# The second half of an output projection by Strassen's products

## The chip, the cores and the metric

One core of one Trainium2 chip runs the whole program in one launch. The metric is device time in microseconds (us) of that core; lower is better. An execution's time is what the device needs for the launch; the span of a profile goes from the first to the last instruction and is a little shorter.

Five engines work side by side, each in the order of its own queue: TensorE (PE; its weight loads are listed as PEld), VectorE (DVE), ScalarE (ACT), GpSimd (POOL) and SyncE (SP), which here only issues DMA transfers. Matmuls write their results into PSUM banks of 512 columns of 4 bytes for 128 partitions; the other engines take them from there.

## What is computed

A decoder trunk of two layers on 512 tokens with 1024 channels, all in float32. Layer 1, where the change is (shortened):

```python
xn = rms_norm(h, norm_mix[1])
proj = gelu(xn @ w_in_odd)                      # 512 x 2048
u, v = proj[:, :1024], proj[:, 1024:]
mix = u * gate(v)                               # position mixing in chunks of 128
h = h + mix @ w_out_odd                         # 512x1024 by 1024x1024: the change is here
hn = rms_norm(h, norm_ffn[1])
h = h + gated_conv_ffn(hn, w_ffn_gate[1], w_ffn_up[1], conv_ffn[1], b_conv_ffn[1], w_ffn_down[1])
out = rms_norm(h, final_norm)
```

## The kernel before

The residual h lies in SBUF as eight tiles `h[0]` to `h[7]` of 128 channels by 512 tokens. A float32 product is made of three matmuls in a rounded format (`fp32r`): each operand is split into a high part (rounded, by ScalarE) and a low part (the rest, by VectorE), and high x high, high x low and low x high are summed in one bank (`mm3`, lines 156 to 159). `parts` (line 149) splits weights in this way. `summed` (line 138) makes the low part in another way: ScalarE writes the negated high part, and a DMA issued by GpSimd adds the raw values onto it.

`mixer1` (line 898) makes layer 1's mixer. Its last steps are these. The group "u1" multiplies the second half of u (banks of 128 tokens by 512 channels); along with it `spatial`, `gated` and `turned` make the gated mix of a head (128 channels) and transpose it on TensorE. `turned(j)` (line 1099) takes the transposed bank, `mT`, into a high part (ScalarE, line 1108) and a low part (VectorE, line 1109) of a tile `mx`: `mix[j]` is channel block j by 512 tokens. Blocks 0 to 3 are turned within "u1", blocks 4 to 7 within the first half of the output projection by the hook `second_half` (line 1163).

The output projection "oo" is one call of `project` (line 303). It makes two halves: half 0 gives `h[0..3]`, half 1 gives `h[4..7]`. A half takes four raw tiles of weights (256 rows by 512 columns each), split by `parts`, and makes 4 row blocks x 8 chunks of the contraction x 3 matmuls = 96 matmuls of 512 columns. For the first four chunks the row blocks alternate, for the last four each row block is finished by itself (`group`, line 161). A finished row block is added to `h[k]` by VectorE (line 315), and `norm.add(k)` prepares it for the FFN: the high and the low part `hg[k]` of h times the gain (ScalarE line 202, VectorE line 203), the square (ScalarE), and the sum of squares (GpSimd, line 213).

Behind it `ffn1` starts: `Ffn.pair_weights` (line 631) fetches and splits four tiles of gate and up weights, `direct` (line 645) multiplies them with `hg` in the order 0, 4, 1, 5, 2, 6, 3, 7, and `turn_residual` (line 1184) transposes h on TensorE for the last part of the kernel (`hT`, two tiles ahead of each pair of row blocks). Meanwhile `block_sums` and `prepare` make the operands of the first feature pair that goes by Strassen's products; the kernel already uses these in its other layers' steps, with `multiply` (line 558) and the table `BANK` (line 554), which says which products go on in one bank.

Buffers that matter here, each a set of slots that come free when the last reader is done: raw weights (tag `raw`, 4), their high and low parts (`whi`, `wlo`, 6 each), PSUM banks for matmuls (7), tag `v` in mixer1 (4 tiles of 2 x 512 columns: first v, then the gated mix `gt`), tag `u` (2), `vn` (4, at the end `mx`), `ws` (1).

The order of the work on each engine is set by a planner at build time: it takes, of what it reckons ready, the instruction that stands first in the program. `behind(a, b)` (line 83) puts a behind b on their engine. Each queue is then strict; a transfer on SP's queue that waits for a slot holds up the transfers behind it.

Of the kernel before, what the change touches and what calls it, by code (L numbers as in the profile page):

```python
# [31 lines left out]
def tile_trunk(ctx: ExitStack, tc: tile.TileContext, x, norm_mix, norm_ffn, final_norm,  # L32
# [3 lines left out]
    nc = tc.nc  # L36
    x = x[0]
# [92 lines left out]
    def fetch(src, a, b, name):  # L130
        raw = wp.tile([P, a, b], F32, tag="raw", bufs=4, name=f"raw_{name}")
        nc.sync.dma_start(raw, src)
        return raw, a, b, name
# [15 lines left out]
    def parts(raw, a, b, name, after=(None, None)):  # L149
        hi = wp.tile([P, a, b], F32R, tag="whi", bufs=6, name=f"whi_{name}")  # L150
        lo = wp.tile([P, a, b], F32R, tag="wlo", bufs=6, name=f"wlo_{name}")
        behind(nc.scalar.activation(hi, raw, AF.Copy), after[1])  # L152
        behind(nc.vector.tensor_tensor(lo, raw, hi.bitcast(F32), ALU.subtract), after[0])  # L153
        return hi, lo
# [31 lines left out]
    h = [cp.tile([P, S], F32, tag=f"h{k}", name=f"h{k}") for k in range(NK)]  # L186
# [116 lines left out]
    def project(name, w, acts, ks, norm, before=None, halves=(0, 1), tail=4):  # L303

        for gi in halves:
            chunks = half_weights(name, w, ks, gi)

            def lhs(k, j):
                hi, lo, n = chunks[k]
                cs = slice(j * P, (j + 1) * P)  # L310
                return hi[:, n, cs], lo[:, n, cs]

            def done(j, ps):
                k = gi * 4 + j
                nc.vector.tensor_tensor(h[k], ps, h[k], ALU.add)  # L315
                if norm is not None:
                    norm.add(k)

            group(f"{name}{gi}", range(4), ks, lhs, lambda k, j: acts[k], tail, done,
                  before if gi == 0 else None)  # L320
# [221 lines left out]

    STEPS = [(0, None, True), (2, (0, 2, 0), False), (4, (0, 2, 1), True)]
    for f in range(6, NF, 4):
        STEPS += [(f, (f - 4, f, 0), False), (f + 2, (f - 4, f, 1), f + 4 < NF)]
# [44 lines left out]
    class Ffn:  # L592
# [38 lines left out]
        def pair_weights(self, order):  # L631

            ch = {}
            for key, half in order:
                name = f"{key}{self.layer}_0_{half}"
                raw = wp.tile([P, 4, 2 * P], F32, tag="raw", bufs=4, name=f"raw_{name}")
                w = (w_ffn_gate if key == "g" else w_ffn_up)[self.layer][:, : 2 * P]
                w = w.rearrange("(h k p) c -> p h k c", h=2, p=P)
                for h_ in range(2):
                    nc.sync.dma_start(raw.rearrange("p (k h) c -> p h k c", h=2)[:, h_],  # L640
                                      w[:, h_, 2 * half : 2 * half + 2])
                ch[key, half] = parts(raw, 4, 2 * P, name)
            return ch

        def direct(self, ch, before):
# [56 lines left out]
        def moving(self, product, kp):  # L702

            if product in (1, 2, 3):
                k = kp if product == 1 else kp + NP
                c = slice(HALF, S) if product == 3 else slice(0, HALF)
                return hg[k][0][:, c], hg[k][1][:, c]
            if product in (6, 7):
                t = self.t23[kp][product - 6]
                return t[:, 0, :], t[:, 1, :]  # L710
            return tuple(t[:, {4: 0, 5: 1}[product], :] for t in self.t41[kp])
# [186 lines left out]
    def mixer1(norm):  # L898
        w = w_in_odd[0]
        with tc.tile_pool(name="m1", bufs=1) as mp:  # L900
# [74 lines left out]
            class InProducts:  # L975
# [19 lines left out]
                def put(self, product, how, at):  # L995
                    self.stat[product] = [how(raw, 2, 512, f"{self.name}_{product}_{n}")
                                          for n, raw in enumerate(self.raw[at])]
# [75 lines left out]
                                                   op0=ALU.mult, op1=ALU.subtract)  # L1073
                vn.append((hi, lo))

            u, gt, mix = {}, {}, {}

            def by_chunk(ap):
                return ap.rearrange("p (n c) -> p n c", c=P)
# [19 lines left out]
            def turned(j):  # L1099
                half, i = j // 4, j % 4  # L1100
                if i == 0:
                    mix["t", half] = [mp.tile([P, 4, S], F32R, tag="vn", bufs=4,
                                              name=f"mx{half}_{n}") for n in range(2)]
                ps = mm_bank(f"mT{j}")
                for t in range(NT):
                    nc.tensor.transpose(ps[:, t * P : (t + 1) * P], gt[j][:, t, :], ident)
                hi, lo = (x[:, i, :] for x in mix["t", half])
                nc.scalar.activation(hi, ps, AF.Copy)
                nc.vector.tensor_tensor(lo, ps, hi.bitcast(F32), ALU.subtract)
                mix[j] = hi, lo  # L1110

            u[0] = mp.tile([P, NT, S], F32, tag="u", bufs=2, name="u0")

# [49 lines left out]
            def second_half(k):  # L1163
                if 1 <= k < 4:
                    for j in ((4,), (5,), (6, 7))[k - 1]:
                        turned(j)

            nxt = Norm("f1", lambda k: prm1("ffn", k))
            project("oo", w_out_odd[0], mix, list(range(NK)), nxt, before=second_half)
            return nxt  # L1170


# [241 lines left out]
    n = ffn0(n)  # L1414
# [32 lines left out]
```

## Time and profile before

| | us |
|---|---|
| median of three runs | 972.78 (971.95 to 972.93) |
| profiled execution | 972.66 |
| its span, first to last instruction | 970.9 |
| TensorE busy in the span | 961.0 (99%) |
| VectorE busy | 812.9 (84%) |
| ScalarE busy | 597.5 (62%) |
| GpSimd busy | 152.0 (16%) |

The granted TensorE clock was 0.998 over the span. Times in the trace count from the start of the span. A row of the timeline shows start, duration, engine, line, operation, the tile written and the tiles read; in square brackets how long the engine sat idle before it, and what ended that. A row of grouped instructions shows the count, busy time and the mean of one in nanoseconds, or minimum, median and maximum. Rows of waits show who waited for whom: total, times, longest. In the table by stretches stand for each engine the busy time and the number of instructions. The durations of matmuls overlap: what counts is the distance from one start to the next.

### The profile page before, as it was taken

The numbers are of one execution on the slowest core, as the hardware profiler recorded it, in microseconds if no ns is written. First come the engines' busy times: TensorE is split into PE (matmuls) and PEld (weight loads), VectorE is DVE, ScalarE is ACT, GpSimd is POOL, SyncE is SP. The second block draws the span as 40 slices with busy tenths as digits, with TensorE's granted clock in tenths as the row PEclk, the third lists the DMA queues.
The fourth block names the chain that finished last, engine by engine and source line by source line (L and its number), as shares of the span: only waits on it lengthen the run. The fifth ranks groups of instructions, "written<-read, shape, count | busy, mean of one in ns | idle before, by whom it ended". The sixth has DMA issues, their size and how long they took to land.

```text
span 970.9 us, 13658 instructions
## 1 busy us (share of the span) xinstructions
PE 961.0 (99%) x4952; PEld 818.6 (84%) x4952; DVE 812.9 (84%) x1387; ACT 597.5 (62%) x895; POOL 152.0 (16%) x173
## 2 busy tenths in 40 slices
PE   9999999999999999999999999999999999999996
PEld 7888888988888888888888888889888888888885
DVE  6887458999898998998878675589998989889897
ACT  5523347765675665765586834587665666656775
POOL 3141023110111010110311001221111011100123
PEclk9999999999999999999999999999999999999999
DMA  7442225776777677774352333167767777668775
GB/s 252 149 137 86 87 88 111 178 180 161 195 175 168 157 174 195 168 176 135 128 153 87 109 109 108 51 136 182 185 142 196 195 174 174 159 162 200 195 154 139
DMA packets 92335, 148.33 MB, mean 153 GB/s; under 512 B 5124, under 2 KB 56300, under 8 KB 92268
## 3 DMA queue, kind: packets, MB, share of 16 engines
q1 hardware_dynamic: 76236, 98.69, 32.1%
q0 software_dynamic: 14256, 46.93, 26.8%
q10 hardware_dynamic: 1776, 1.84, 0.6%
q8 instruction: 39, 0.64, 0.3%
q14 instruction: 28, 0.23, 0.1%
HBM read 98.42 MB, written 2.10 MB: 104 GB/s over the span
## 4 chain that ended last, share of the span: by engine, by line
PE 94%; DVE 3%; DMA 1%; issue 1%; ACT 0%; POOLq 0%; DVEq 0%; POOL 0%
PE dn L158 3%; PE dn L159 3%; PE dn L157 3%; PE d L158 3%; PE d L157 3%; PE d L159 3%; PE vu_a L1026 2%; PE gu L157 2%; PE gu L159 2%; PE oo L159 2%; PE oo L157 2%; PE gu L158 2%; PE oe L159 1%; PE oe L158 1%; PE oo L158 1%; PE oe L157 1%
## 5 line engine op out<-in xcount | busy, mean ns | idle before, releaser
L144 POOL DMA_DIRECT2D wlo_g<-raw_g x20 | 17.2, 862 | 318.8 <-ACT wlo_g L142 118.3
L617 DVE SCALAR_TENSOR_TENSOR c<-rows,prm,c 128x512 f32<-128x512 f32 x88 | 65.3, 744 | 1.6 <-ACT c L615 1.4
L158 PE MATMUL dn<-wlo_dn,a_hi 128*128 128x512 f32 x144 | 56.2, 390 | 0.0
L158 PE MATMUL d<-a_lo,whi_d 128*128 128x512 f32 x144 | 56.2, 390 | 0.0
L159 PE MATMUL dn<-whi_dn,a_lo 128*128 128x512 f32 x144 | 56.2, 390 | 0.0
L159 PE MATMUL d<-a_hi,wlo_d 128*128 128x512 f32 x144 | 56.1, 390 | 0.0
L157 PE MATMUL d<-a_hi,whi_d 128*128 128x512 f32 x144 | 56.1, 390 | 0.0
L157 PE MATMUL dn<-whi_dn,a_hi 128*128 128x512 f32 x144 | 56.1, 390 | 0.0
L731 ACT ACTIVATE whi_a<-raw_g 128x512 fp32r<-128x512 f32 x20 | 12.6, 632 | 61.3 <-PE g_10e L571 9.0
L213 POOL TENSOR_TENSOR ssq_f<-ssq_f,sq_f 128x512 f32<-128x512 f32 x14 | 19.8, 1411 | 142.4 <-issue 102.0
L142 ACT ACTIVATE wlo_g<-raw_g 128x1024 fp32r<-128x1024 f32 x20 | 21.2, 1062 | 27.5 <-PE g_2e L581 8.8
L202 ACT ACTIVATE hg<-h,prm 128x512 fp32r<-128x512 f32 x24 | 17.3, 721 | 33.1 <-DVE h L315 33.1
L615 ACT ACTIVATE c<-rows,prm 128x512 f32<-128x512 f32 x44 | 31.4, 715 | 9.8 <-DVE rows L828 9.6
L625 ACT ACTIVATE s<-c,prm 128x512 f32<-128x512 f32 x44 | 31.4, 716 | 6.2 <-DVE c L617 6.1
L1201 DVE SCALAR_TENSOR_TENSOR y<-dn,small,y 128x512 f32<-128x512 f32 x40 | 28.0, 749 | 8.1 <-PE dn L159 8.1
L203 DVE SCALAR_TENSOR_TENSOR hg<-h,prm,hg 128x512 fp32r<-128x512 f32 x24 | 22.6, 944 | 11.9 <-ACT hg L202 11.9
L159 PEld LDWEIGHTS dn<-whi_dn,a_lo 128*128 128x128 f32 x144 | 27.0, 188 | 5.7
L159 PEld LDWEIGHTS d<-a_hi,wlo_d 128*128 128x128 f32 x144 | 27.0, 188 | 5.7
L153 DVE TENSOR_TENSOR wlo_dn<-raw_dn,whi_dn 128x1024 fp32r<-128x1024 f32 x18 | 22.0, 1224 | 11.7 <-ACT whi_dn L152 10.6
L157 PEld LDWEIGHTS d<-a_hi,whi_d 128*128 128x128 f32 x144 | 27.1, 188 | 5.4
L157 PEld LDWEIGHTS dn<-whi_dn,a_hi 128*128 128x128 f32 x144 | 27.1, 188 | 5.4
L158 PEld LDWEIGHTS dn<-wlo_dn,a_hi 128*128 128x128 f32 x144 | 27.0, 188 | 5.4
(1060 smaller groups left out, 3261.6 us busy)
## 6 DMA issues: line engine op xcount, KB each, us to landing
raw_g<-in_w_ffn_gate_dram SPq DMA_DIRECT2D x40, 512.0 KB, 3.8
raw_u<-in_w_ffn_up_dram SPq DMA_DIRECT2D x40, 512.0 KB, 4.3
raw_dn<-in_w_ffn_down_dram SPq DMA_DIRECT2D x22, 512.0 KB, 6.0
wlo_g<-raw_g POOLq DMA_DIRECT2D x20, 512.0 KB, 4.6
wlo_u<-raw_u POOLq DMA_DIRECT2D x20, 512.0 KB, 6.4
raw_d<-in_w_ffn_down_dram SPq DMA_DIRECT2D x18, 512.0 KB, 4.1
wlo_s12g<-s12g POOLq DMA_DIRECT2D x18, 512.0 KB, 6.3
wlo_s34g<-s34g POOLq DMA_DIRECT2D x18, 512.0 KB, 5.7
```

The lines of the kernel that those rows point to most:

```text
L142: first = nc.scalar.activation(lo, raw, AF.Copy, scale=-1.0)
L153: behind(nc.vector.tensor_tensor(lo, raw, hi.bitcast(F32), ALU.subtract), after[0])
L157: nc.tensor.matmul(ps, lhs[0], rhs[0], start=start, stop=False)
L158: nc.tensor.matmul(ps, lhs[0], rhs[1], start=False, stop=False)
L159: nc.tensor.matmul(ps, lhs[1], rhs[0], start=False, stop=stop)
L203: nc.vector.scalar_tensor_tensor(hg[k][1], h[k], g, hg[k][0].bitcast(F32), op0=ALU.mult, op1=ALU.subtract)
L213: nc.gpsimd.tensor_tensor(self.ssq, self.ssq, sq, ALU.add)
L615: nc.scalar.activation(c, t[:, 0:S], AF.Copy, scale=prm("cf", ft))
L617: self.last_conv = nc.vector.scalar_tensor_tensor(c, t[:, i : S + i], prm("cf", i * NF + ft), c, op0=ALU.mult, op1=ALU.add)
L625: self.last_silu = nc.scalar.activation(s, c, AF.Silu, bias=self.prm("bf", ft))
L1026: nc.tensor.matmul(banks[at], lhs[l], rhs[r], start=first, stop=end, skip_group_check=True)
L1201: return nc.vector.scalar_tensor_tensor(dst, ps, ffn.cols[:, t : t + 1], dst, op0=ALU.mult, op1=ALU.add)
```

## The change

The first half of "oo" stays a call of `project`, now with `halves=(0,)`. The second half (channels 512 to 1023 of the output, contraction 1024, tokens 512) is cut into 2 x 2 blocks: output channels 256+256, contraction 512+512, tokens 256+256. It is made by seven block products (Strassen's scheme in Winograd's form) in place of eight, each of 2 row blocks x 4 chunks x 3 matmuls of 256 columns.

- `turned` also copies each transposed block whole to a float32 tile `whole` (tag `v`, two blocks to a tile).
- `sums_of(q)`, called for q = 0, 1 in the hook ahead of the fifth and sixth chunk of the first half, makes the sums and differences of the mix's blocks in place on VectorE (`block_sums_of`, four instructions), splits two of them into the tiles `hg[4..7]`, which are free at that time (high part by ScalarE, low part by VectorE), and the other two into a tile `t43` (tag `u`) with an accumulating DMA.
- `project_blocks` fetches the same weights as four raw blocks, makes their sums and differences in place on VectorE with one spare tile (`ws`), and splits seven block operands by `parts` in the order in which the products use them: 1, 2, 6, 5, 7, 3, 4.
- Each product is added to the halves of `h[4..7]` that need it. Products 1, 6, 7 and 4 go on summing in one bank (`a`), product 2 has a bank of its own, and product 3, which shares the bank of product 5 elsewhere, gets a new one here (`banks[i].pop("e")`). `norm.add` follows products 3 and 4.
- In `pair_weights` the low parts of the first two FFN weight tiles are ordered behind product 5's last addition on VectorE.

```diff
+    def block_sums_of(y0, y1):
+        t3, t1, t2, t4 = y1[:, :, HALF:], y0[:, :, HALF:], y0[:, :, :HALF], y1[:, :, :HALF]
+        nc.vector.tensor_tensor(t3, t3, t1, ALU.subtract)
+        nc.vector.tensor_tensor(t1, t1, t2, ALU.subtract)
+        nc.vector.tensor_tensor(t2, t2, t3, ALU.add)
+        nc.vector.tensor_tensor(t4, t4, t2, ALU.subtract)
+
+    first_weights_after = [None]
+
+    def project_blocks(name, w, acts, sums, norm, spare):
+        raw = {}
+        for i, j in ((0, 0), (1, 0), (1, 1), (0, 1)):
+            raw[i, j] = fetch(w[i * 512 : (i + 1) * 512, 512 + j * HALF : 512 + (j + 1) * HALF]
+                              .rearrange("(k p) c -> p k c", p=P), 4, HALF, f"{name}_{i}{j}")
+        stat = {}
+
+        def put(product, how, at):
+            r, a, b, n = raw[at]
+            stat[product] = how(r, a, b, f"{n}_{product}")
+
+        def to(at, x, y, op):
+            nc.vector.tensor_tensor(raw[at][0], raw[x][0], raw[y][0], op)
+
+        a11, a12, a21, a22, s1 = (0, 0), (1, 0), (0, 1), (1, 1), "s1"
+        raw[s1] = spare, 4, HALF, f"{name}_s1"
+        put(1, parts, a11)
+        put(2, parts, a12)
+        to(s1, a21, a22, ALU.add)
+        to(a21, a11, a21, ALU.subtract)
+        to(a11, s1, a11, ALU.subtract)
+        put(6, parts, a11)
+        to(a12, a12, a11, ALU.subtract)
+        put(5, parts, s1)
+        put(7, parts, a21)
+        put(3, parts, a12)
+        put(4, parts, a22)
+
+        def moving(product, kp):
+            if product in (1, 2, 3):
+                c = slice(HALF, S) if product == 3 else slice(0, HALF)
+                return tuple(x[:, c] for x in acts[kp + (0 if product == 1 else NP)])
+            return sums[product](kp)
+
+        onto = {1: [(0, 0)], 2: [(0, 0)], 6: [(0, 1)], 5: [(0, 1), (2, 1)], 7: [(2, 1)],
+                3: [(0, 1)], 4: [(2, 0)]}
+        banks = ({}, {})
+        for product in (1, 2, 6, 5, 7, 3, 4):
+            for i in range(2):
+                hi, lo = stat[product]
+                c = slice(i * P, (i + 1) * P)
+                if product == 3:
+                    banks[i].pop("e")
+                ps = multiply(banks[i], f"{name}_{product}{i}", product,
+                              lambda kp: (hi[:, kp, c], lo[:, kp, c]),
+                              lambda kp: moving(product, kp))
+                for row, half in onto[product]:
+                    d = h[4 + i + row][:, half * HALF : (half + 1) * HALF]
+                    ins = nc.vector.tensor_tensor(d, ps, d, ALU.add)
+                if product == 5:
+                    first_weights_after[0] = ins
+                if product in (3, 4):
+                    norm.add(4 + i + 2 * (product == 4))
...
-                ch[key, half] = parts(raw, 4, 2 * P, name)
+                ch[key, half] = parts(raw, 4, 2 * P, name,
+                                      after=(None if half else first_weights_after[0], None))
...
+                if i % 2 == 0:
+                    whole[half].append(mp.tile([P, 2, S], F32, tag="v", bufs=4, name=f"mr{j}"))
+                nc.scalar.copy(whole[half][-1][:, i % 2, :], ps)
...
+                elif k in (4, 5):
+                    sums_of(k - 4)
+
+            def sums_of(q):
+                y0, y1 = whole[0][q], whole[1][q]
+                block_sums_of(y0, y1)
+                for n in range(2):
+                    hi, lo = hg[4 + 2 * q + n]
+                    nc.scalar.activation(hi, y0[:, n, :], AF.Copy)
+                    nc.vector.tensor_tensor(lo, y0[:, n, :], hi.bitcast(F32), ALU.subtract)
+                t = mp.tile([P, 2, 2, S], F32R, tag="u", bufs=2, name=f"t43_{q}")
+                nc.scalar.activation(t[:, 1], y1, AF.Copy, scale=-1.0)
+                nc.gpsimd.dma_start(t[:, 1], y1, accum_op=ALU.add)
+                nc.scalar.activation(t[:, 0], y1, AF.Copy)
+                t43.append(t)
...
-            project("oo", w_out_odd[0], mix, list(range(NK)), nxt, before=second_half)
+            project("oo", w_out_odd[0], mix, list(range(NK)), nxt, before=second_half, halves=(0,))
...
+            project_blocks("oo1", w_out_odd[0], mix,
+                           {6: lambda kp: tuple(x[:, :HALF] for x in hg[4 + kp]),
+                            5: lambda kp: tuple(x[:, HALF:] for x in hg[4 + kp]),
+                            4: lambda kp: late(kp, slice(0, HALF)),
+                            7: lambda kp: late(kp, slice(HALF, S))}, nxt,
+                           mp.tile([P, 4, HALF], F32, tag="ws", bufs=1, name="oo_s1"))
```

`late(kp, c)` gives the high and low part of `t43` for chunk kp.

More of the change, by code (lines that the diff above doesn't have):

```diff
@@ L1074, in v_normed @@
                 vn.append((hi, lo))
-            u, gt, mix = {}, {}, {}
+            u, gt, mix, whole = {}, {}, {}, ([], [])
             def by_chunk(ap):
@@ L1166, in second_half, with late @@
                         turned(j)
-            nxt = Norm("f1", lambda k: prm1("ffn", k))
-            project("oo", w_out_odd[0], mix, list(range(NK)), nxt, before=second_half)
+                elif k in (4, 5):
+                    sums_of(k - 4)
+            t43 = []
+            def sums_of(q):
[10 more added lines that the diff above has]
+                t43.append(t)
+            nxt = Norm("f1", lambda k: prm1("ffn", k))
+            project("oo", w_out_odd[0], mix, list(range(NK)), nxt, before=second_half, halves=(0,))
+            def late(kp, c):
+                return tuple(t43[kp // 2][:, i, kp % 2, c] for i in range(2))
+            project_blocks("oo1", w_out_odd[0], mix,
[4 more added lines that the diff above has]
+                           mp.tile([P, 4, HALF], F32, tag="ws", bufs=1, name="oo_s1"))
             return nxt
```

## The prediction

> **What bounds the kernel now.** I read the chain that ended last first, then what TensorE waited for over the whole run.
>
> ```profile
> PE 94%; DVE 3%; DMA 1%; issue 1%; ACT 0%; POOLq 0%; DVEq 0%; POOL 0%
> ...
> PE clock L61 <- DVE idle L56: 1.3, 1, 1.3
> PE z L441 <- ACT hg L409: 0.3, 1, 0.3
> PE g_10a L571 <- DVE rows L804: 0.3, 1, 0.3
> PE u_10a L571 <- DVE kept L804: 0.2, 1, 0.2
> ```
>
> 94% of the chain is TensorE, and the four rows are all the waits of PE that the trace shows, 2.1 us. All lie ahead of the change: the first two at the start, the last two between 200 and 380 us, in layer 0 (the same view of 680 to 940 us has no row). So time is the sum of the matmuls' pitches, and an edit gains only what it takes off PE, as long as PE goes on being fed. Next, the timeline of PE around the edited half and at the first place where matmuls of 256 columns run.
>
> ```profile
> 599.98 0.39 PE L157 MATMUL oo<-mx,whi_oo 128*128 128x512 f32 x1
> ...
> 621.75 1.04 PE L1187 MATMUL hT<-ident,h 128*128 128x128 f32 x8
> ...
> 648.53 0.40 PE L581 MATMUL g_2a<-hg,whi_a 128*128 128x256 f32 x2
> ...
> 660.04 0.40 PE L581 MATMUL u_2b<-hg,whi_u 128*128 128x256 f32 x2
> ```
>
> The second half of "oo" is 96 matmuls (8 chunks of the contraction, 4 row blocks, 3 each) of 512 columns; counted back from the first residual transpose at 621.75 it starts at 599.98: 21.77 us, a pitch of 0.2268. From 648.53 to 660.04 lie eight products of 12 matmuls of 256 columns: 11.51 us over 96, a pitch of 0.1199. The 0.39 and 0.40 us in the rows are latencies and overlap.
>
> How full each engine is, stage by stage (second group of u; first half of oo; second half; the first products of the FFN):
>
> ```profile
> core 0: us, PE busy (x) PEld busy (x) DVE busy (x) ACT busy (x) POOL busy (x), PEclk, DMA share, GB/s
> 553.00:576.20 23.20, 23.20 (x113) 19.05 (x113) 17.38 (x26) 11.24 (x16) 0.00 (x0) 1.00 0.27 91
> 576.20:600.50 24.30, 24.30 (x117) 20.19 (x116) 14.60 (x19) 10.80 (x17) 2.22 (x2) 1.00 0.28 87
> 600.50:621.90 21.40, 21.40 (x97) 17.68 (x96) 11.28 (x13) 8.53 (x13) 5.20 (x5) 1.00 0.32 98
> ...
> 648.40:662.00 13.60, 13.60 (x115) 13.56 (x114) 13.60 (x22) 11.57 (x20) 0.86 (x1) 1.00 0.61 155
> ```
>
> PE is full in all four. VectorE idles 24.30-14.60 = 9.70 us and 21.40-11.28 = 10.12 us in the two halves of oo: 19.8 us. ScalarE idles 13.5 and 12.9 us. That idle time is what the change spends.
>
> **The change, part by part.**
>
> *TensorE.* Out: 96 matmuls at 0.2268. In: 7 products x 2 row blocks x 4 chunks x 3 = 168 of 256 columns at 0.1199 = 20.14 us. Gain 21.77-20.14 = 1.63 us: an eighth of the columns goes, but two 256-column matmuls take 0.2398 where one of 512 takes 0.2268. The transposes mT and hT stay as they are. The pitch is bounded below by half the wide one, 0.1134 (19.05 us, gain 2.72), and I see nothing that would put it above 0.1199; I take 0.1199, which eight products in a row show with changes of bank and of weights among them. In that stage the weight loads are busy 13.56 of 13.60 us, against 17.68 of 21.40 in oo, which is why half the columns don't cost half.
>
> The Trainium skill (TensorE: Matmul & The Clock Gate, "Back-to-back issue gap") gives an isolated gap of columns over 2.4 plus 2.5 ns, 215.8 and 109.2 ns, by which the gain would be an estimated 2.4 us. Both rows here are longer (226.8 and 119.9), the narrow one by more, so the measured pitches decide; what is left of that rule is the rival of the short pitch below.
>
> *VectorE.* The durations, from groups that keep shapes apart:
>
> ```profile
> L752 DVE TENSOR_TENSOR s12g<-raw_g,raw_g 128x512 f32<-128x512 f32 x20 | 13.7, 686 | 9.1 <-DMA raw_g<-in_w_ffn_gate_dram 9.1
> L1001 DVE TENSOR_TENSOR raw_vu<-raw_vu,raw_vu 128x1024 f32<-128x1024 f32 x8 | 9.6, 1220 | 0.0
> L804 DVE TENSOR_TENSOR kept<-u_20a,kept 128x256 f32<-128x256 f32 x10 | 4.2, 420 | 0.9 <-PE u_20a L574 0.8
> ...
> L1109 DVE TENSOR_TENSOR mx<-mT,mx x8: 675/680/691, 564.3 to 587.4; 128x512 fp32r<-128x512 f32 x8
> L1108 ACT ACTIVATE mx<-mT x8: 581/598/601, 562.9 to 586.6; 128x512 fp32r<-128x512 f32 x8
> L152 ACT ACTIVATE whi_oo<-raw_oo x8: 1043/1056/1065, 546.7 to 589.1; 128x1024 fp32r<-128x1024 f32 x8
> L153 DVE TENSOR_TENSOR wlo_oo<-raw_oo,whi_oo x8: 1212/1220/1226, 547.8 to 590.2; 128x1024 fp32r<-128x1024 f32 x8
> L315 DVE TENSOR_TENSOR h<-oo,h x8: 678/692/692, 592.0 to 623.1; 128x512 f32<-128x512 f32 x8
> ```
>
> Added: two calls of four block sums, 8 x 0.69 = 5.5; four low parts of those sums, 4 x 0.68 = 2.7; four sums and differences of weights, 4 x 1.22 = 4.9; seven low parts of weights in place of four, 3 x 1.22 = 3.7; 16 additions of half a bank at 0.42 in place of four of 0.69, 6.7-2.8 = 3.9. Together 20.7 us into 19.8-1.6 = 18.2 us of idle time. It doesn't fit by itself, so cover matters:
>
> ```profile
> 576.29 1.23 DVE L153 TENSOR_TENSOR wlo_oo<-raw_oo,whi_oo 128x1024 fp32r<-128x1024 f32 x1 [5.73 <-ACT whi_oo L152]
> 577.44 2.73 DVE L1095 SCALAR_TENSOR_TENSOR gt<-gt,prm,u 128x512 f32<-128x512 f32 x4
> ```
>
> Ahead of 576.29 VectorE sat idle 5.73 us, waiting for ScalarE's copy, which waited for a weight buffer.
>
> ```profile
> L132 SPq DMA_DIRECT2D raw_oo<-in_w_out_odd_dram x8: 367/368/422, 538.8 to 568.2; - x8
> ...
> DMA to landing us min/median/max: 3.2/3.4/3.6
> ```
>
> The new sums of raw weights need no such buffer: the last of oo's weights, issued at 568.2, are there 3.4 us later, so two of the four (s1, then a21) can run before 576: 2.4 us. And the second of the rows above starts 0.08 us before the first ends; over some 41 instructions until the third product that is 3 us more than the durations say. So VectorE is full, but not overfull.
>
> What must be ready when, with 2.88 us a product from 599.98: product 1 at 599.98, 2 at 602.9, 6 at 605.7, 5 at 608.6, 7 at 611.5, 3 at 614.4, 4 at 617.3, the FFN at 620.1. The narrow point is product 6: it goes on in the bank of product 1, so its first matmul waits until VectorE has added product 1 to h, and it needs the low parts of all four sums and of its own weights. Until 605.7, 29.5 us from 576.2, VectorE has its old work, 14.60 plus about 1 (the low parts of the FFN's weights at 600.8 and 601.9 are put behind product 5's addition and go), and of the new: 5.5+2.7+4.9, up to three low parts of products 7, 3, 4 if they are queued ahead (3.7), two additions (0.8): 17.6. Sum 33.2. Less 2.4 done before 576, it is 1.3 us too late by durations and 1.7 us early with the overlap; 3.7 us late with neither. The ends are 0 and 3.7 us of wait; I take 0, since product 4's weights can't be split before product 1 has released its buffer at 602.9 and so fall behind or beside the additions, and both small reserves are rows of this stage.
>
> *Weight buffers and queues.*
>
> ```profile
> 575.20 1.06 ACT L152 ACTIVATE whi_oo<-raw_oo 128x1024 fp32r<-128x1024 f32 x1 [0.67 <-PE u L159]
> ...
> 582.32 1.06 ACT L152 ACTIVATE whi_oo<-raw_oo 128x1024 fp32r<-128x1024 f32 x1 [2.00 <-PE oo L158]
> ...
> 589.08 1.06 ACT L152 ACTIVATE whi_oo<-raw_oo 128x1024 fp32r<-128x1024 f32 x1 [1.86 <-PE oo L158]
> ...
> 621.10 0.61 ACT L731 ACTIVATE whi_a<-raw_g 128x512 fp32r<-128x512 f32 x1
> ```
>
> The six split-weight buffers come free as before: products 1 and 2 take those of 575.20 and after, 6 and 5 those released by oo at 582.3 and 589.1, 7 and 3 at the end of the first half (about 600), 4 product 1's (602.9); each is 11 us or more ahead of its product but for 1 and 2, which keep their old times. The FFN's gate and up weights follow products 2, 6, 5, 7 (605.7 to 614.4); the first two low parts, ordered behind product 5's last addition (about 612.2), end near 615, 5 us before 620.1.
>
> ```profile
> 602.04 0.37 SPq L132 DMA_DIRECT2D raw_g<-in_w_ffn_gate_dram  x1
> 603.17 0.37 SPq L132 DMA_DIRECT2D raw_u<-in_w_ffn_up_dram  x1
> 607.74 0.37 SPq L132 DMA_DIRECT2D raw_g<-in_w_ffn_gate_dram  x1
> 613.18 0.37 SPq L132 DMA_DIRECT2D raw_u<-in_w_ffn_up_dram  x1
> ...
> raw_g<-in_w_ffn_gate_dram SPq DMA_DIRECT2D x40, 512.0 KB, 3.8
> wlo_s12g<-s12g POOLq DMA_DIRECT2D x18, 512.0 KB, 6.3
> ```
>
> The raw weights now live until their sums are split. SP's queue, in order, waits near 601 for the second FFN load, and behind it stand two more loads and these four of the next feature pair, which go to about 613 to 618. They land 4 us later, by 622; ScalarE's first use was at 621.10, PE's at 648.53. Hidden by 26 us; without that cover PE would lose the 1 us.
>
> *ScalarE and GpSimd.* Eight copies of the turned mix (0.60 each, four of them in the u group), three more high parts (1.06), four high parts of sums (0.6) and two pairs for products 7 and 4 (4 x 1.06): 14.6 us in 12+13.5+12.9 idle. The two accumulating DMAs (512 KB, about 6.3 us to land) start once the sums stand, about 590 to 597, and are due at 611.5. Cost 0, covered by 8 us. A bank more for product 3: oo's four banks are released by 601, so 3 of 7 are spare. Cost 0.
>
> Sum: profiled execution 972.66 (span 970.9 and 1.76 around it) - 1.63 = 971.03. That execution lies 0.12 under the median of the three, 972.78, from which the same gain gives 971.15. Forecast 971.1.
>
> **The rivals.**
>
> *VectorE becomes the bound* (slower). Its waits in the stage of oo:
>
> ```profile
> DVE wlo_oo L153 <- ACT whi_oo L152: 9.4, 3, 5.7
> DVE hg L203 <- ACT hg L202: 4.8, 6, 0.8
> DVE wlo_u L153 <- ACT whi_u L152: 4.2, 1, 4.2
> DVE h L315 <- PE oo L159: 3.7, 7, 0.6
> ```
>
> If the 4.8 and 3.7 us, answers it awaits from ScalarE and PE between its own instructions, stay unfilled because its queue is strict, it needs 25.9 old + 20.7 + 8.5 = 55.1 us where 43.9 (45.5 of the stage less the gain) and the 5.7 ahead make 49.6: 5.5 us late, first at product 6's bank, then at the sums and additions behind. 972.66-1.63+5.5 = 976.5. For it: the sum of durations is 94% of what there is. Against: at 600.8 two low weights were put exactly into such waits. It decides from 1.6 us (gain lost) and 3.6 us (slower by 0.2%).
>
> *The gain is eaten* (about no change): product 6 waits the 1.3 us worked out above, or 2: 972.4 to 973.0.
>
> *Short pitch*: 256 columns at 0.1134 gives 972.66-2.72 = 969.9. For it: in oo the weight loads are not the limit, 17.68 of 21.40 us. Against: the eight products quoted, where they are.
>
> **How the numbers follow.** Changes below 0.2%, 1.95 us, can't be told from none: the lines are 970.83 and 974.73. Forecast 0.60 (own range 970.5 to 971.8; the three runs before spread over 1 us, so about 0.20 of it falls under 970.83); VectorE as the bound 0.22, nearly all above 974.73; gain eaten 0.11; short pitch 0.07. Faster 0.20+0.07 = 0.27; slower 0.22; the rest, 0.51, within. The range, 970.2 to 975.5, leaves out the short pitch and half of the VectorE case, 2 in 10.
>
> **What would show it.** Right: 168 matmuls of 256 columns at 0.120 with no wait of PE in them; the first residual transpose at 620.1; VectorE busy over 90% there with low weights filling its old waits; the next pair's loads issued 4 to 11 us later and nobody waiting. Wrong: a wait of PE for an addition at the start of product 6, for the low part of a sum, or for the FFN's first low weights; a pitch other than 0.12; residual transposes at 620 but the same end, which would mean that the time is lost again behind.

## The result

The changed kernel takes 974.32 us (median of 22 runs, 973.57 to 975.26) beside 972.63 us before (22 runs on the same chip, 971.95 to 974.03): a ratio of 1.0017, 95% interval 1.0011 to 1.0024, or 1.1 to 2.3 us more. The forecast was 971.1 us, 1.6 us less than before; the time lies in the range of 970.2 to 975.5, with the sign the other way round. The prediction drew its line at 0.2%; this change is smaller, but its interval leaves out 1.

### The profile page after: what moved, and what is told of

It reads as the page before. It is cut to its first block, busy times and chain, and to the rows that moved or that the text cites. A ratio compares the mean times of both kernels' runs of the same rounds, so it can differ in the third digit from the quotient of the medians.

```text
span 972.0 us, 13875 instructions
## 1 busy us (share of the span) xinstructions
PE 960.2 (99%) x5024; PEld 821.1 (84%) x5024; DVE 832.9 (86%) x1418; ACT 610.1 (63%) x914; POOL 155.2 (16%) x175
## 3 DMA queue, kind: packets, MB, share of 16 engines
q10 hardware_dynamic: 1776, 1.84, 0.6%
## 4 chain that ended last, share of the span: by engine, by line
PE 92%; DVE 3%; ACT 2%; DMA 1%; issue 1%; POOL 0%; DVEq 0%; POOLq 0%; ACTq 0%
PE dn L158 3%; PE d L158 3%; PE dn L159 3%; PE dn L157 3%; PE d L159 3%; PE d L157 3%; PE vu_a L1092 2%; PE oe L159 1%; PE oe L157 1%; PE oe L158 1%; PE u_4a L646 1%; PE vu_e L1092 1%; PE dn_a L1391 1%; PE g_2a L646 1%; PE u_2a L646 1%; PE g_10a L636 1%
## 5 line engine op out<-in xcount | busy, mean ns | idle before, releaser
L203 DVE SCALAR_TENSOR_TENSOR hg<-h,prm,hg 128x512 fp32r<-128x512 f32 x24 | 24.8, 1034 | 8.6 <-ACT hg L202 8.6
L266 ACT ACTIVATE a_hi<-s 128x512 fp32r<-128x512 f32 x40 | 24.9, 627 | 11.1 <-PE d L159 7.7
```

Source lines behind the costliest of these rows:

```text
L203: nc.vector.scalar_tensor_tensor(hg[k][1], h[k], g, hg[k][0].bitcast(F32), op0=ALU.mult, op1=ALU.subtract)
L266: nc.scalar.activation(hi, src, AF.Copy, scale=scale)
```

## The profile after

The profiled execution took 973.75 us (span 972.0). The waits of TensorE, in all of the run (who waited for whom: total, times, longest):

```profile
PE clock L61 <- DVE idle L56: 1.3, 1, 1.3
PE g_2a L646 <- ACT rows L882: 1.1, 1, 1.1
PE gu L157 <- ACT y L1285: 0.6, 1, 0.6
PE oo_10a L646 <- DVE h L604: 0.5, 1, 0.5
PE z L441 <- ACT hg L409: 0.3, 1, 0.3
```

The first and the last lie at the run's start, as before. The other three are new, and none is large. Where they lie in time shows TensorE's timeline (start, duration, engine, line; in brackets the idle time before it and what ended that), here of the changed kernel; the second row is product 6's first matmul, the last is the first matmul of the next stage, "dn".

```profile
599.60 0.40 PE L646 MATMUL oo_10a<-mx,whi_oo 128*128 128x256 f32 x2
...
605.97 0.47 PE L646 MATMUL oo_10a<-hg,whi_oo 128*128 128x256 f32 x2 [0.46 <-DVE h L604]
...
620.44 0.38 PE L1283 MATMUL hT<-ident,h 128*128 128x128 f32 x2
...
625.00 0.50 PE L157 MATMUL gu<-hg,whi_u 128*128 128x512 f32 x1 [0.57 <-ACT y L1285]
...
648.08 0.40 PE L646 MATMUL g_2a<-hg,whi_a 128*128 128x256 f32 x2
...
659.40 0.51 PE L646 MATMUL g_2a<-t,whi_s34g 128*128 128x256 f32 x2 [1.10 <-ACT rows L882]
...
669.58 0.40 PE L157 MATMUL dn<-whi_dn,a_hi 128*128 128x512 f32 x1
```

In the kernel before, "dn" begins here:

```profile
668.68 0.40 PE L157 MATMUL dn<-whi_dn,a_hi 128*128 128x512 f32 x1
```

With the starts that the prediction quotes this gives three stages: the edited half (to the first residual transpose), the direct products (to the first "g_2a") and the FFN's first products (to "dn"). The first half of "oo" takes 23.62 us in both kernels, and behind "dn" all stages agree within 0.02 us.

| us | before | after | difference |
|---|---|---|---|
| edited half | 21.77 | 20.84 | -0.93 |
| direct products | 26.78 | 27.64 | +0.86 |
| first products of the FFN | 20.15 | 21.50 | +1.35 |
| together | 68.70 | 69.98 | +1.28 |

So the seven products did gain, and more was lost in three waits than they gained: 20.84 is 20.15 us of products and 0.69 us at product 6, and 0.69 + 0.86 + 1.35 = 2.90 us against a gain of 1.62. By stages each wait costs 0.2 to 0.3 us more than its row of waits says. The 1.28 us lie within the interval of 1.1 to 2.3 us around the 1.69 between the medians; the profiled execution of the changed kernel is the second fastest of its 22.

The engines in the second group of u, the first half of oo, the edited half, the direct products and the first products (busy time and instructions of PE, PEld, DVE, ACT and POOL):

```profile
553.00:575.80 22.80, 22.80 (x112) 18.72 (x111) 19.51 (x27) 12.86 (x20) 0.00 (x0) 1.00 0.29 93
575.80:599.60 23.80, 23.80 (x114) 19.78 (x113) 23.15 (x32) 17.69 (x28) 2.79 (x3) 1.00 0.29 64
599.60:620.40 20.80, 20.34 (x169) 20.16 (x168) 18.26 (x27) 10.02 (x12) 5.64 (x4) 1.00 0.49 150
620.40:648.10 27.70, 27.13 (x143) 22.65 (x142) 19.92 (x40) 22.87 (x44) 10.61 (x10) 1.00 0.48 100
648.10:669.60 21.50, 20.40 (x170) 20.20 (x169) 20.73 (x33) 16.09 (x26) 2.58 (x3) 1.00 0.58 151
```

VectorE is busy for 23.15 of 23.80 us in the first half (14.60 of 24.30 before) and 18.26 of 20.80 in the edited half. It is full, and yet keeps up: what was to be found out is whether its load or the order of its queue and of ScalarE's makes the three waits.

**Product 6.** VectorE's timeline:

```profile
600.93 2.86 DVE L153 TENSOR_TENSOR wlo_oo<-raw_oo,whi_oo 128x1024 fp32r<-128x1024 f32 x2
603.71 1.78 DVE L203 SCALAR_TENSOR_TENSOR hg<-h,prm,hg 128x512 fp32r<-128x512 f32 x1
605.41 0.41 DVE L604 TENSOR_TENSOR h<-oo_10a,h 128x256 f32<-128x256 f32 x1
```

Product 6 goes on in product 1's bank and needs the addition at 605.41. Product 1's first row block is done at about 601.2 (in e9 below, where nothing stands ahead of it, the addition runs 1.63 us after the products begin). But ahead of the addition stand the low weights of products 7 and 3, which are not due before 611, and the low part of hg.

**The direct products.** ScalarE's timeline, and the loads of the next feature pair in SP's queue:

```profile
613.92 0.37 SPq L132 DMA_DIRECT2D raw_g<-in_w_ffn_gate_dram  x1
615.38 0.89 SPq L132 DMA_DIRECT2D raw_u<-in_w_ffn_up_dram  x1
...
618.31 0.37 SPq L132 DMA_DIRECT2D raw_u<-in_w_ffn_up_dram  x1
```

```profile
618.34 0.62 ACT L797 ACTIVATE whi_a<-raw_g 128x512 fp32r<-128x512 f32 x1
620.44 0.63 ACT L797 ACTIVATE whi_a<-raw_u 128x512 fp32r<-128x512 f32 x1 [1.49 <-DMA raw_u<-in_w_ffn_up_dram]
620.98 0.71 ACT L202 ACTIVATE hg<-h,prm 128x512 fp32r<-128x512 f32 x1
...
624.38 2.01 ACT L1285 COPY y<-hT 128x512 f32<-128x512 f32 x4
626.28 0.74 ACT L746 ACTIVATE t<-h,prm 128x512 f32<-128x512 f32 x1
```

ScalarE stands for 1.49 us at the split of the next pair's first raw_u, issued at 615.38, which lands 5.0 us later. Behind it in its queue are three of the norm's hg and their squares, and only then the copies y that empty the banks of the residual transposes. The direct products wait for such a bank.

**The first products.** VectorE waits for a DMA:

```profile
639.55 0.69 DVE L818 TENSOR_TENSOR s12g<-raw_g,raw_g 128x512 f32<-128x512 f32 x1 [2.29 <-DMA t<-t]
...
649.86 0.68 DVE L730 TENSOR_TENSOR rows<-gu,rstd_f 128x512 f32<-128x512 f32 x1
```

Weight sum s12g is written into a tile of the ring "sum", of which there are three, and which the block sums t of the FFN use too (one t for each of four pairs of channel blocks). By the bracket, the tile comes free when an accumulating DMA t<-t has read it. There are six of these, three for pair 0 and three for pair 1; GpSimd issues the last four in a row, and the very last, issued at 634.7, lands 4.6 us later:

```profile
632.45 3.52 POOL L765 DMA_DIRECT2D t<-t  x4 [0.93 <-ACT t L766]
```

In the kernel before they went out in four groups, the first and last of which are these, and s12g waited for nothing; behind pair 2's low parts (first row of the second view) it followed within 0.4 us:

```profile
628.80 1.78 POOL L699 DMA_DIRECT2D t<-t  x2 [2.21 <-ACT t L698]
...
637.25 0.86 POOL L699 DMA_DIRECT2D t<-t  x1 [0.59 <-ACT t L700]
```

```profile
637.81 1.36 DVE L732 TENSOR_TENSOR t<-t,t 128x512 fp32r<-128x512 f32 x3 [0.68 <-ACT t L731]
...
639.49 0.68 DVE L752 TENSOR_TENSOR s12g<-raw_g,raw_g 128x512 f32<-128x512 f32 x1
...
646.69 0.69 DVE L664 TENSOR_TENSOR rows<-gu,rstd_f 128x512 f32<-128x512 f32 x1 [0.64 <-PE gu L159]
```

The DMAs weren't earlier there: the last one, issued at 637.25, landed 4.1 us later, when s12g had been running since 639.49. So s12g was written into another tile. In the built programs it has, before, the address of pair 2's t, which is split by ScalarE and VectorE without a DMA; in the changed kernel it has that of pair 1's t, which the last three DMAs read, and it stands ahead of pair 2's low parts in VectorE's queue. Which tile a request gets is settled when the program is built.

s12g itself starts hardly later, 8.53 us ahead of the first g_2a (639.55 and 648.08) instead of 9.04. What costs is that VectorE stands still ahead of it with other work queued behind, pair 2's low parts too (e11 below). Behind s12g everything on VectorE is late: the rows of the direct products, which began 1.84 us ahead of the first g_2a (646.69 and 648.53), now begin 1.78 us behind it, with them ScalarE's silu, and behind that in ScalarE's queue the copy that frees the bank of g_2a:

```profile
655.67 1.28 ACT L690 ACT_TABLE_LOAD   x1 [0.65 <-DVE c L682]
656.97 1.34 ACT L690 ACTIVATE s<-c,prm 128x512 f32<-128x512 f32 x2
658.21 0.35 ACT L882 COPY rows<-g_2e 128x256 f32<-128x256 f32 x1
658.99 0.35 ACT L882 COPY rows<-g_2a 128x256 f32<-128x256 f32 x1
```

TensorE goes on at 659.40, when that copy is done.

## The experiments

Twelve kernels, each beside runs of the kernel before on the same chip (972.66 to 972.80 us there). All that start from the changed kernel have 23.62 us in the first half and the old lengths behind "dn", but for 0.44 us more in one later stage of e8's profile. "A" is the edited half, "B" the direct products, "C" the first products, from the profiled execution; the ratio is to the kernel before.

| kernel | us | ratio, 95% interval | A | B | C |
|---|---|---|---|---|---|
| changed kernel | 974.32 | 1.0017 [1.0011, 1.0024] | 20.84 | 27.64 | 21.50 |
| e1 no block sums | 973.47 | 1.0009 [1.0000, 1.0017] | 20.15 | 27.82 | 21.04 |
| e2 raw_g's and raw_u's splits later | 973.90 | 1.0011 [1.0003, 1.0020] | 20.84 | 26.81 | 21.80 |
| e3 addition first | 973.58 | 1.0008 [0.9999, 1.0017] | 20.15 | 27.49 | 21.49 |
| e4 = e2 + e3 | 972.96 | 1.0005 [0.9996, 1.0014] | 20.15 | 26.81 | 21.77 |
| e5 = e4, product 3 before 7 | 974.53 | 1.0019 [1.0009, 1.0028] | A + B 48.28 | | 21.91 |
| e6 = e4 + fourth sum tile | 971.11 | 0.9984 [0.9975, 0.9993] | 20.15 | 26.81 | 20.15 |
| e7 before, rows late | 972.68 | 1.0001 [0.9992, 1.0009] | 21.76 | 26.78 | 20.16 |
| e8 = e5 + fourth sum tile | 972.65 | 1.0000 [0.9991, 1.0009] | A + B 48.28 | | 20.15 |
| e9 = e4, first sum early | 971.33 | 0.9983 [0.9974, 0.9993] | 20.15 | 26.81 | 20.15 |
| e10 before + fourth sum tile | 972.36 | 0.9997 [0.9988, 1.0007] | 21.77 | 26.78 | 20.15 |
| e11 changed + fourth sum tile | 973.22 | 1.0000 [0.9991, 1.0010] | 20.84 | 28.01 | 20.15 |
| e12 no squares added | 972.83 | 1.0000 [0.9990, 1.0009] | 20.15 | 27.73 | 20.75 |

(Before: 21.77, 26.78 and 20.15. In e5 and e8 the first residual transposes come among the products, so only A + B is given; e4 has 46.96. For e7 and e10 A is counted back as in the prediction.) The stages reproduce to some 0.02 us from one profile to the next where nothing is changed, so they tell edits apart that medians 0.2 us apart can't. In the built programs s12g has pair 1's tile in the changed kernel, e1 to e5 and e12, the runs with a C above 20.16; it has pair 2's in the kernel before, e7 and e9, and pair 0's in the four runs with a fourth tile.

**e1: is VectorE's load the cause?** The copies `whole`, the block sums and t43 are left out; products 6, 5, 7 and 4 read plain blocks.

```diff
-                nc.scalar.copy(whole[half][-1][:, i % 2, :], ps)
...
-                elif k in (4, 5):
-                    sums_of(k - 4)
...
-                           {6: lambda kp: tuple(x[:, :HALF] for x in hg[4 + kp]),
+                           {6: lambda kp: tuple(x[:, :HALF] for x in mix[4 + kp]),
```

> Leaves out the sums of the mix's blocks: no whole copies, no block sums, no splits of them; products 6, 5, 7 and 4 read plain blocks of the mix, so the output is not the reference's. TensorE's work is that of the change. It takes 8.2 us from VectorE and 11.4 us from ScalarE, all before product 6. Queue theory (three waits of PE from the order on strict queues, the last two from ScalarE standing 1.5 us at a late raw weight): the wait at product 6 (0.6 us) goes, the ones at gu (0.7) and at the FFN's first products (1.2) stay: about 973.7. Rival, too much vector work in the stage: all waits go, about 971.0.

973.47 us. VectorE has 6 to 7 us less to do up to the edited half, which removes the wait at product 6 and 0.46 us of C; B is as long as ever. So 1.15 of the 2.90 us goes with the work and the rest doesn't: the theory by which the amount of work makes all three waits falls.

**e2: the splits of the next pair's first raw_g and raw_u behind the norm's last hg on ScalarE.**

```diff
-                self.halves(w[0][:, i], w[1][:, i], raws[key, 0][0][:, :, :P])
+                self.halves(w[0][:, i], w[1][:, i], raws[key, 0][0][:, :, :P],
+                            self.norm.last_hi if layer == 1 and f == 2 else None)
```

> ScalarE's splits of the first raw weights of the next feature pair (whi_a) put behind the last normalised row, so that a late load of these weights holds up nothing of oo. Queue theory: ScalarE doesn't stand 1.5 us at 619, the wait at gu (0.7 us) goes and most of the 1.2 us at the FFN's third g product: 972.3 to 973.0, product 6 still waits 0.6. Rival (too much vector work): the waits move, within 0.3 us of 974.3.

B falls to 26.81, the old length within 0.03 us: the two splits, one of which waits for its load, are the cause of the second wait. But 0.3 of the 0.83 us goes into C, and the time missed what was expected: the third wait isn't an echo of the second.

**e3: the low weights of products 7, 3 and 4 behind product 1's last addition on VectorE.**

```diff
-        put(7, parts, a21)
-        put(3, parts, a12)
-        put(4, parts, a22)
...
+            if product == 2:
+                for late_, at in ((7, a21), (3, a12), (4, a22)):
+                    put(late_, lambda *raw_: parts(*raw_, after=(ins, None)), at)
```

> VectorE's low weights of products 7, 3 and 4 put behind the addition of product 1. Queue theory: product 6 starts without a wait, 0.6 us less than 974.3, 973.7, the other two waits stay. Rival: the low weights are late instead, product 7 or 3 waits, no gain.

A is 20.15 us, the seven products without a wait: the addition now runs as soon as TensorE is done with the bank (as in e9, which has this edit too):

```profile
601.56 0.43 DVE L604 TENSOR_TENSOR h<-oo_10a,h 128x256 f32<-128x256 f32 x1 [0.22 <-PE oo_10a L646]
```

The order on VectorE is enough to make or remove the first wait.

**e4: both.**

> Both orders of the two runs before it. Queue theory: 971.5 to 972.4, up to 1.1 us under the kernel before. Rival: within 0.3 us of 974.3.

972.96 us, above what was expected. A and B are as they should be; C stays at 21.77. The theory of two waits was a wait short.

**e5: product 3 ahead of product 7**, so that the rows of h which product 3 completes, and the norm on them, come earlier; the rival to it was the sum tile.

```diff
-        for product in (1, 2, 6, 5, 7, 3, 4):
+        for product in (1, 2, 6, 5, 3, 7, 4):
```

> Both orders of the run before, and product 3 made ahead of product 7, so that rows 4 and 5 of h are complete 2.9 us earlier and no longer 4.3 us of four rows end the stage. What is left there is 1.6 us between the first g product of the FFN and its first down matmul (21.77 against 20.15 in the kernel before). Theory of the late rows: ScalarE's work for four rows of h within the last 4.3 us of oo pushes the first block sums of the FFN 4 us back, and with them a chain of DMAs for which VectorE waits (3.1 us before s12g); rows earlier take most of it: 20.2 to 21.0 in that stage, 971.4 to 972.2 in all. Rival (too few tiles for sums, or too much VectorE work, whatever the rows do): 21.6 to 21.8, 973.0.

It made things worse. C stays (21.91), s12g waits as long, and TensorE has a new wait:

```profile
PE oo_11a L646 <- DVE h L604: 1.1, 1, 1.1
```

Product 4 goes on in product 7's bank and now follows it at once, so product 7's addition is no longer covered by product 3. The theory of the late rows falls, for this order at least.

**e6: e4 with four tiles "sum" in layer 1** (and, to have the memory, one buffer in place of two for the spread norm).

```diff
-            t = self.ap.tile([P, 4, HALF], F32, tag="sum", bufs=3, name=f"t{n}")
+            t = self.ap.tile([P, 4, HALF], F32, tag="sum", bufs=3 + 1 * self.layer, name=f"t{n}")
```

> Both orders, and in layer 1 four tiles for block sums in place of three, so that s12g needn't wait for the release of the second one (the memory comes from a second tile for the spread factor that isn't needed). Theory of the late rows: the block sums are as late as before, so only the wait of s12g goes: 20.6 to 21.4 in the stage. Rival (too few tiles): 20.2, 971.4 in all.

971.11 us, with no wait of TensorE left but the two at the run's start:

```profile
PE clock L61 <- DVE idle L56: 1.3, 1, 1.3
PE z L441 <- ACT hg L409: 0.3, 1, 0.3
```

**e7: the late rows put into the kernel before** (its last rows of h come 1.36 us apart, as the new ones do).

```diff
-            group(f"{name}{gi}", range(4), ks, lhs, lambda k, j: acts[k], tail, done,
+            group(f"{name}{gi}", range(4), ks, lhs, lambda k, j: acts[k],
+                  2 if name == "oo" and gi == 1 else tail, done,
```

> The kernel before, with one number changed: in oo's second half only the last two chunks of the contraction are done row by row, so the four rows end 1.36 us apart in place of 2.72, as in the changed kernel (1.44). No other work. Theory of the late rows: PE waits appear in the gu stage or at the FFN's first products, 0.8 to 2 us: 973.4 to 974.6. Rival: within 0.3 us of the kernel before.

972.68 us and no wait but the run's first: how the rows are spaced costs nothing in the kernel before, where s12g has pair 2's tile.

**e8: e5 and e6 together.**

> Both orders, product 3 ahead of 7, four sum tiles. Theory: all waits gone, 971.1 (the products' gain of 1.6 us alone). Rival (VectorE's total work): a wait of 0.5 us or more stays at the FFN's first products, 971.6 or more.

972.65 us, not the 971.1 expected. C is 20.15 with the fourth tile here too, and e5's wait for product 7 stays (1.1 us): the two add up and don't mix.

**e9: e4 with the first block sum of the FFN emitted ahead of the direct products**, three tiles as before.

```diff
                 ch = self.pair_weights([("g", 0), ("u", 0), ("g", 1), ("u", 1)])
+                if self.layer == 1:
+                    self.sum_tile(0)
                 rest = self.direct(ch, first)
```

(`sum_tile` is the first part of `block_sums`, as far as the DMAs.)

> The kernel of e4, with one more edit: in layer 1 the first block-sum tile of the FFN (t of pair 0) is emitted ahead of the direct products, so that ScalarE writes it before it copies the transposed residual. If s12g waits because the six accumulating DMAs of the block sums start late and bunched (t of pair 0 starts 5.8 us after the first transpose in the changed kernel, 0.4 us in the kernel before), then t starts within 1 us of the first transpose, the DMAs spread, s12g waits under 1 us, the stage from g_2a to dn takes 20.2 us instead of 21.8, and the kernel takes 971.2 to 971.8 us. Rival: the place of s12g in VectorE's queue, ahead of the low parts of the next sum, makes the wait whatever the start of t: the stage stays over 21 us and the time is 972.6 to 973.2 us.

The third wait goes without any memory: 971.33 us. ScalarE writes t ahead of the copies y, and GpSimd's issues are spread again; these are the last two:

```profile
622.38 0.71 ACT L765 ACTIVATE t<-h,prm 128x512 f32<-128x512 f32 x1
622.99 2.01 ACT L1297 COPY y<-hT 128x512 f32<-128x512 f32 x4
```

```profile
636.27 1.75 POOL L757 DMA_DIRECT2D t<-t  x2 [2.93 <-ACT t L756]
```

t starts 2.3 us behind the first residual transpose (620.08), not within the 1 us expected, and that is enough. But the spread isn't the reason: the last DMA, issued at 637.1, lands 3.4 us later, when s12g has begun (640.22). The edit put s12g behind pair 2's low parts and into pair 2's tile, as in the kernel before, so it starts later than in the changed kernel against the first g_2a (6.67 us ahead, not 8.53) and yet waits for nothing. This run changes tile and place together; e11, where s12g keeps its place, says that the wait for the tile is the loss.

**e10: the kernel before with four tiles.**

> The kernel before, with four block-sum tiles in layer 1 instead of three (and one buffer less for the spread norm). If the fourth tile only takes away a wait that the change brought, nothing moves: 972.7 us, with 20.15 us from g_2a to dn, as before. Rival: four tiles are worth something by themselves, and part of the 1.6 us by which e6 beats the kernel before has nothing to do with the change: 971.1 to 972.0 us.

972.36 us, interval across 1, C 20.15 as before: the fourth tile is worth nothing without the change, and what e6 gains is the change's.

**e11: the changed kernel with four tiles and nothing else.**

> The changed kernel, with four block-sum tiles in layer 1 and nothing else. If the three waits are separate, the first two stay (20.84 us for the half, 27.64 to g_2a) and the third goes (20.15 to dn): 974.3 - 1.35 = 973.0 us. Rival: the third wait is what is left over from the split of raw_u that ScalarE stands at, and goes on with it: over 21 us to dn and 974 us.

C 20.15, A 20.84, 973.22 us, as expected for three separate waits. s12g, at the same place in the queue, waits for nothing:

```profile
637.81 0.66 DVE L818 TENSOR_TENSOR s12g<-raw_g,raw_g 128x512 f32<-128x512 f32 x1
```

B is 0.37 us longer here (28.01): ScalarE stood 1.87 us at raw_u instead of 1.49. That wait depends on a load, and need not be the same in each execution.

**e12: what GpSimd has to do with the first wait.** The seven additions of squares for the FFN's norm are left out.

```diff
-                nc.gpsimd.tensor_tensor(self.ssq, self.ssq, sq, ALU.add)
+                if self.name != "f1":
+                    nc.gpsimd.tensor_tensor(self.ssq, self.ssq, sq, ALU.add)
```

> The changed kernel without GpSimd's seven additions of squares for the norm of layer 1's FFN (so the norm's scale is not the reference's); VectorE's queue has the same order. If product 6 waits 0.7 us because VectorE and GpSimd slow each other there, hg's low part falls from 1.04 us on average to 0.75, the two low weights ahead of product 1's addition from 2.86 to 2.4, the wait of product 6 goes below 0.1 us, the half takes 20.2 us instead of 20.84 and the kernel 973.6 us. Rival: the order alone makes the wait and the slow instructions are slow for another reason: durations and the half as before, 974.2 us.

VectorE's three instructions of above, in the same order:

```profile
600.42 2.36 DVE L153 TENSOR_TENSOR wlo_oo<-raw_oo,whi_oo 128x1024 fp32r<-128x1024 f32 x2
602.70 0.75 DVE L203 SCALAR_TENSOR_TENSOR hg<-h,prm,hg 128x512 fp32r<-128x512 f32 x1
603.36 0.42 DVE L605 TENSOR_TENSOR h<-oo_10a,h 128x256 f32<-128x256 f32 x1
```

From the first to the addition pass 2.94 us, against 4.48 with GpSimd at work (600.93 to 605.41), and TensorE's wait at product 6 is gone (A 20.15). So two things stand behind that wait, and each alone suffices to remove it: the place of the low weights (e3) and the neighbour (e12). That C fell to 20.75 was not expected; s12g ran 18.56 us after the first transpose in place of 19.11, and why is not shown.

## Why the prediction failed, step by step

- **TensorE: right.** 168 matmuls of 256 columns take 20.15 us without a wait (e3, e4, e6, e9); 20.14 was forecast. The rival of the short pitch falls.
- **VectorE's sum: right.** Its busy time over the run rose by 20.0 us, from 812.9 to the third number of this row; 20.7 were forecast, and it fits, 97% full in the first half of oo. The two sums of weights that were to run ahead of that stage do, and the second group of u is busy for 19.51 - 17.38 = 2.1 us more.

```profile
PE 960.2 (99%) x5024; PEld 821.1 (84%) x5024; DVE 832.9 (86%) x1418; ACT 610.1 (63%) x914; POOL 155.2 (16%) x175
```

- **Product 6, "I take 0": wrong, within its bounds of 0 and 3.7.** It cost 0.69 us. The step reckoned whether the work due before 605.7 fits, and put up to three low weights ahead of product 1's addition as part of that load; the reserve for it was taken from the overlap of VectorE's instructions. The reason given for 0 speaks of product 4's weights alone; those did fall behind the addition (605.75), but those of 7 and 3 stood ahead of it. What decides is when one instruction comes in a strict queue: the addition could have run at about 601.2 and ran at 605.41. And the instructions ahead of it took 1.5 us more than in e12, without GpSimd's additions. The trace before had a hint: from 600.5 to 605.7 VectorE was busy 4.34 us, 2.4 of them the two low weights that went, so "about 1" of old work was about 2, as hg's low part took 1.78 us there.
- **SP's queue, "Hidden by 26 us": wrong.** The loads go out at 613.92 to 618.31, as forecast, and raw_u is there by 620.4. The price was read from TensorE's first use of those weights, at 648.53. The first to meet them is ScalarE, which is not on the path; but three hg and the copies y stand behind the split in its queue, and those empty the bank that TensorE stands waiting for at 625.00. 0.86 us in place of 0 (e2).
- **The third wait: no step at all.** The largest loss, 1.35 us, sits 20 to 40 us behind the edit, in a ring of three tiles that the diff doesn't touch and the prediction doesn't mention. VectorE stands still for 2.29 us until a DMA gives up the tile that s12g now gets, and one tile more takes the whole loss away (e11). The change delivers h later against the copies y: t of pair 0 starts 626.28 - 620.44 = 5.84 us behind the first transpose instead of 0.39 in the kernel before (622.14 - 621.75). An earlier t brings the old tile and place back (e9); what it is in the change that gives s12g another tile stays open.

```profile
622.14 0.71 ACT L680 ACTIVATE t<-h,prm 128x512 f32<-128x512 f32 x1
```

- **Banks, weight buffers, t43: right,** no wait for any of them.
- **The rivals.** "VectorE becomes the bound" isn't what happened: with all of VectorE's new work in place e6 and e9 are faster than before. "The gain is eaten" had the right place, product 6, for half as much as it named, and knew neither of the other two. The first line of what would show the forecast wrong, "a wait of PE for an addition at the start of product 6", and the last, "the time is lost again behind", are what the profile shows. That the time lies within the range is luck: its upper part was there for VectorE as the bound.

With the three waits gone the kernel takes 971.11 us, and the forecast of 971.1 was the time of that kernel, not of this one. e6 and e9 beat the kernel before by 1.6 and 1.5 us, with intervals that leave out 1; e9 needs no memory for it.

## What to carry to other kernels

A delayed transfer is priced at the first instruction that waits for it on any strict queue, and from there at what is queued behind that instruction, not at TensorE's first use of the data. Before forecasting a gain of 0.2%, list the rings of tiles that the next stages share with DMAs, and see which tile each request gets in the built program and what releases it: the largest loss here sat in a ring that the edit doesn't touch, where one request changed its tile. And where a low part that isn't due yet can be put behind an addition that a bank waits for, say so in the order: it cost an ordering edge and brought 0.69 us.

## What the runs showed of the hardware

VectorE's instructions with two operands in SBUF and GpSimd's additions of squares slow each other. The low part of hg (128x512) over the window from 576 to 626 us, minimum, median and maximum in ns; first the changed kernel, then e12 without GpSimd's additions:

```profile
L203 DVE SCALAR_TENSOR_TENSOR hg<-h,prm,hg x8: 742/1042/1781, 595.0 to 625.8; 128x512 fp32r<-128x512 f32 x8
```

```profile
L203 DVE SCALAR_TENSOR_TENSOR hg<-h,prm,hg x8: 743/749/756, 594.9 to 623.4; 128x512 fp32r<-128x512 f32 x8
```

GpSimd pays as well: an addition of squares takes 1.29 us with no such instruction beside it for most of its time (first row, of e10) and 2.23 us next to the hg of 603.71, which takes 1.78 (second row, of the changed kernel):

```profile
600.50 1.29 POOL L213 TENSOR_TENSOR ssq_f<-ssq_f,sq_f 128x512 f32<-128x512 f32 x1 [1.43 <-ACT sq_f L212]
```

```profile
602.71 2.23 POOL L213 TENSOR_TENSOR ssq_f<-ssq_f,sq_f 128x512 f32<-128x512 f32 x1 [1.15 <-ACT sq_f L212]
```

The Trainium skill (SBUF — State Buffer, "SBUF: two separate sides") says that VectorE and GpSimd share one pair of ports, held for a whole instruction by whichever takes it first, and that a VectorE instruction with two inputs in SBUF contends for it with a GpSimd instruction that reads SBUF. The direction agrees: VectorE lost 1.03 us there and GpSimd 0.94, while an addition with one input in PSUM keeps its length beside GpSimd (0.41 or 0.42 us elsewhere; in e9 0.43 us at 601.56, quoted above, under this pair of additions, which goes on to 601.90):

```profile
598.88 3.02 POOL L213 TENSOR_TENSOR ssq_f<-ssq_f,sq_f 128x512 f32<-128x512 f32 x2 [1.59 <-ACT sq_f L212]
```

Whether one waits for the other's whole instruction, no run here shows. In the kernel before the low part of hg has the same worst case (1,778 ns), but nothing is due behind it.
